# A hybrid decoder layer in Strassen products: weight sums on GpSimd, snapshots on VectorE, third products one pair later, last HGRN pieces between early products

## The chip, the cores and the metric

The kernel runs on one core of a Trainium2 chip. The metric is the device time of one execution in microseconds; the time before is the median of three runs. The engines go by the profile's names: PE is TensorE's matmuls, PEld its weight loads, DVE VectorE, ACT ScalarE, POOL GpSimd, SP SyncE, which here issues nearly all DMAs. Each engine works through its own queue in order, and an instruction that has to wait holds up what is queued behind it.

## The reference

One decoder layer on 1024 tokens of width 1024, all in float32. Three token mixers (an HGRN2 recurrence `o_a`, sliding-window attention `o_b`, attention to a memory `o_c`) read projections of h; each result goes through its own weight and a gate, and the sum through `w_out`:

```python
z = h @ w_in[layer]
...
gates = jax.nn.sigmoid(gl.astype(jnp.float32).reshape(B, S, N_BRANCHES, D_MODEL))
merged = (gates[:, :, 0] * (o_a @ w_branch_hg[layer])
          + gates[:, :, 1] * (o_b @ w_branch_swa[layer])
          + gates[:, :, 2] * (o_c @ w_branch_mem[layer]))
mix = merged @ w_out[layer]
h = layer_norm(alpha * h + mix, ln1_g[layer], ln1_b[layer])
ff = jnp.square(jax.nn.relu(h @ w_up[layer])) @ w_down[layer]
h = layer_norm(alpha * h + ff, ln2_g[layer], ln2_b[layer])
```

The change concerns two stages: the part of `h @ w_in` that makes the three gates and HGRN's output gate (the gate stage), and the three products `o @ w_branch` with their gates (the branch stage).

## The kernel before

**Products.** A float32 matrix is held as two parts, a high one that ScalarE casts (`split`, L77) and a low one, the rest, that GpSimd or VectorE subtracts (L78). A product of matrices is high times high, high times low and low times high. The large products use Strassen's scheme in Winograd's form: a weight of two 128x1024 pieces gives four quarter matrices, the activation gives seven operands `xs[1]` to `xs[7]` by sums of its quarters (`combine`, L200 to L210), and seven block products take the place of eight. `prod` (L285) is one block product: four k-steps of three matmuls of 128x512, twelve in all, into a PSUM bank. In the profile operands 1 and 2 lie in tiles X, 3 and 5 in O, 4 in T, 6 in MG and 7 in BT; weights in W, raw loads in R, PSUM banks in pz (three), ps (three) and pt (two). There are four R and four W buffers.

**A pair.** `prepare` (L328) loads two raw weight pieces and makes four sums of their halves on VectorE (`add`, L301), between them the splits of w2, w4 and w3, and of w1 where products 1 and 2 have not been made ahead. The sums are chained: a later one reads what an earlier one wrote. `run` (L341) then issues five or seven products. Bank pz takes product 1 (w1), 6 (w4) and 7 (w3) on top of each other; after each a copy of the running value is kept, by ScalarE (`snap`, L297), or by VectorE where a copy of product 1 is reloaded and added (`plus`). Bank pt takes product 5 (w2), is read by `emit(3)`, and takes product 3 (w3) on top for `emit(2)`. Bank ps takes product 4, and product 2 for `emit(0)`. So the third product on pt must wait until VectorE has read pt.

**Early products.** `two` (L318) makes products 1 and 2 of a weight ahead of the pairs; they need operands 1 and 2 alone. In the gate stage (L409 to L415) there are EARLY_Z = 10 of them, with `x_rest` (L219) between them, which loads pieces of x and makes operands 3 to 7 on VectorE; product 1's copy is stored to DRAM and reloaded. Sixteen pairs follow, the first ten with five products. In the branch stage (L888 to L914) each of three branches begins with EARLY_B = 3 of them, whose pz banks are held, then come four pairs (five products in three, seven in the last). `load_op` (L742) loads and splits the operands 3 to 7 of the branch, two loads of 512 KB for each, and operands 1 and 2 of the next branch at its end. In the first branch `job` (L422) also makes the operands of HGRN's output with `combine` on GpSimd, one job after each pair.

**Emit.** In the branches an `emit` (L860 to L886) reads the PSUM bank with the copy (VectorE, L301), loads the gate, multiplies (L874 in the first branch, L876 later) and adds to the running sum (L301).

**The HGRN tail.** Each head of HGRN is a row of steps; `heads[7][3]`, `heads[6][4]` and `heads[7][4]` (L833 to L835) are the last of a half: a head's output product with its mask, and two ends with a normalisation on VectorE and transposes on PE.

**What sets the order.** A tile scheduler orders each engine's instructions from the program's order, the dependences and the buffers; the queues that come out are those shown with the change.

## Time and profile before

| | us |
|---|---|
| median of three runs (2227.44 to 2231.4) | 2228.95 |
| the profiled execution | 2228.37 |
| its span, first to last instruction | 2226.6 |
| gate stage, early products (56.0 to 145.8) | 89.8 |
| gate stage, five-product pairs (145.8 to 274.3) | 128.5 |
| first branch (1136.3 to 1235.2) | 98.9 |
| second branch (1235.2 to 1336.4) | 101.2 |
| third branch (1336.4 to 1434.9) | 98.5 |

The stretches were read from PE's timeline. In a row of a timeline, consecutive matmuls of one kind are joined (x12 is one product); what stands in brackets is the idle time of the engine ahead of it and the instruction whose end released it. Matmul ends are modelled, so the distance from one start to the next says more than the length of a row.

### The profile page before, as it was taken

To read this page: it belongs to the slowest core of one execution; us is meant where nothing else is said; L and a number is where in the kernel's file an instruction comes from. 1 tells how busy PE (TensorE), PEld (TensorE's weight loads), DVE (VectorE), ACT (ScalarE), POOL (GpSimd) and SP (SyncE) were. 2 spreads that over 40 slices of the span, in tenths; PEclk is the share of its full clock that TensorE was granted. 3 is DMA by queue.
4 is the path that set the end of the run, shared out by engine and by line. 5 is a ranking of instruction groups with operands and counts; after the bars stand their busy time and mean duration, and the time that the engine had idled before them with its cause. 6 is when DMAs were issued, how large, how long until landed. Compare 5 with 4: busy or idle time off the path is not lost.

```text
span 2226.6 us, 27069 instructions
## 1 busy us (share of the span) xinstructions
PE 2061.4 (93%) x9906; PEld 1681.2 (76%) x9906; DVE 1418.6 (64%) x2218; ACT 883.7 (40%) x1546; POOL 938.2 (42%) x430
## 2 busy tenths in 40 slices
PE   8889999999999999999978797898989999999987
PEld 8667788777789877779956575777778887788865
DVE  5634435576445577575574778845556655588898
ACT  5433333444444344454321433413544455433321
POOL 2533333211222222423355545634533334777674
PEclk9999999999999999999989898999899999999998
DMA  8554434322234323554355646435556546744322
GB/s 286 192 170 144 135 105 128 115 85 83 98 108 129 114 91 113 186 202 166 110 189 212 239 146 218 155 113 180 194 183 228 187 155 211 289 152 151 114 86 76
DMA packets 153781, 347.03 MB, mean 156 GB/s; under 512 B 13696, under 2 KB 31280, under 8 KB 153648
## 3 DMA queue, kind: packets, MB, share of 16 engines
q1 hardware_dynamic: 153040, 343.19, 46.4%
q10 hardware_dynamic: 608, 2.11, 0.3%
q8 instruction: 78, 1.28, 0.2%
q14 instruction: 55, 0.45, 0.1%
HBM read 254.01 MB, written 91.24 MB: 155 GB/s over the span
## 4 chain that ended last, share of the span: by engine, by line
PE 40%; DVE 7%; POOL 6%; DMA 5%; issue 5%; ACT 2%; SPq 0%; POOLq 0%; DVEq 0%; ACTq 0%
PE pz L62 20%; PE ps L62 12%; PE pt L62 7%; POOL W L78 2%; DMA R<-d_o 1%; DMA R<-in_w_up_dram 1%; DVE R L301 1%; DMA R<-in_w_b_dram 1%; DVE S L876 1%; DVE T L301 1%; POOL BT L78 1%; ACT W L77 1%; DVE G L301 1%; DMA S<-d_z 1%; POOL MG L78 0%
## 5 line engine op out<-in xcount | busy, mean ns | idle before, releaser
L78 POOL TENSOR_TENSOR W<-R,W 128x1024 fp32r<-128x1024 f32 x200 | 494.3, 2473 | 931.5 <-ACT W L77 890.1
L77 ACT CAST W<-R 128x1024 fp32r<-128x1024 f32 (+1 forms) x289 | 283.9, 983 | 378.4 <-DVE R L301 182.1
L62 PE MATMUL pz<-X,W 128*128 128x512 f32 x1344 | 338.2, 404 | 15.8 <-POOL W L78 5.6
L62 PEld LDWEIGHTS pz<-X,W 128*128 128x128 f32 x1344 | 256.4, 194 | 75.6 <-POOL W L78 9.5
L62 PE MATMUL pt<-O,W 128*128 128x512 f32 x1056 | 273.9, 409 | 36.4 <-DVE G L301 22.4
L62 PEld LDWEIGHTS pt<-O,W 128*128 128x128 f32 x1056 | 204.7, 197 | 93.1 <-DVE G L301 26.5
L62 PE MATMUL pz<-O,W 128*128 128x512 f32 x816 | 197.2, 395 | 0.0
L301 DVE TENSOR_TENSOR R<-R,R 128x512 f32<-128x512 f32 x132 | 102.6, 782 | 139.6 <-POOL W L78 113.3
L62 PEld LDWEIGHTS pz<-O,W 128*128 128x128 f32 x816 | 150.5, 188 | 32.2
L62 PE MATMUL pz<-MG,W 128*128 128x512 f32 x528 | 134.6, 400 | 15.1 <-ACT W L77 13.3
L62 PE MATMUL pz<-BT,W 128*128 128x512 f32 x528 | 131.5, 398 | 14.0 <-DVE G L301 13.6
L62 PEld LDWEIGHTS pz<-MG,W 128*128 128x128 f32 x528 | 101.6, 194 | 40.5 <-ACT W L77 15.5
L62 PE MATMUL ps<-X,W 128*128 128x512 f32 x528 | 129.2, 393 | 2.3 <-DVE G L301 2.3
L62 PEld LDWEIGHTS pz<-BT,W 128*128 128x128 f32 x528 | 99.3, 191 | 40.8 <-ACT W L77 15.8
L62 PE MATMUL ps<-T,W 128*128 128x512 f32 x528 | 129.1, 392 | 0.1
L62 PEld LDWEIGHTS ps<-X,W 128*128 128x128 f32 x528 | 99.9, 190 | 24.3 <-DVE G L301 3.1
L62 PEld LDWEIGHTS ps<-T,W 128*128 128x128 f32 x528 | 99.9, 189 | 21.7 <-ACT T L77 0.6
L78 DVE TENSOR_TENSOR W<-R,W 128x512 fp32r<-128x512 f32 (+1 forms) x91 | 92.8, 1020 | 22.1 <-ACT W L77 21.8
L78 POOL TENSOR_TENSOR MG<-R,MG 128x1024 fp32r<-128x1024 f32 (+1 forms) x39 | 100.6, 2582 | 12.6 <-ACT MG L77 12.6
L78 POOL TENSOR_TENSOR BT<-R,BT 128x1024 fp32r<-128x1024 f32 x31 | 82.8, 2673 | 51.5 <-ACT BT L77 51.5
L301 DVE TENSOR_TENSOR T<-pt,G 128x512 f32<-128x512 f32 x64 | 44.0, 688 | 66.9 <-PE pt L62 62.4
L297 ACT COPY G<-pz 128x512 f32<-128x512 f32 x92 | 53.4, 581 | 78.1 <-PE pz L62 78.1
(289 smaller groups left out, 3712.5 us busy)
## 6 DMA issues: line engine op xcount, KB each, us to landing
R<-d_ff SPq DMA_DIRECT2D x49, 512.0 KB, 3.7
R<-in_w_up_dram SPq DMA_DIRECT2D x42, 512.0 KB, 4.1
R<-in_w_gate_dram SPq DMA_DIRECT2D x34, 512.0 KB, 4.0
R<-in_w_b_dram SPq DMA_DIRECT2D x33, 512.0 KB, 4.3
d_ff<-T SPq DMA_DIRECT2D x56, 256.0 KB, 3.1
d_z<-T SPq DMA_DIRECT2D x54, 256.0 KB, 2.5
R<-d_o SPq DMA_DIRECT2D x26, 512.0 KB, 3.8
d_o<-G SPq DMA_DIRECT2D x48, 256.0 KB, 2.3
```

Source lines behind the costliest of these rows:

```text
L62: nc.tensor.matmul(o, lhsT=l, rhs=r, start=start, stop=stop, skip_group_check=more)
L77: (hi_copy or nc.scalar.copy)(hi, src)
L78: (lo_eng or nc.gpsimd).tensor_tensor(out=lo, in0=src, in1=f32(hi), op=ALU.subtract)
L297: nc.scalar.copy(t, o)
L301: nc.vector.tensor_tensor(out=o, in0=a_, in1=b_, op=op)
L876: nc.vector.scalar_tensor_tensor(out=th, in0=th, scalar=1.0, in1=v, op0=ALU.add, op1=ALU.mult)
```

## The change

In the gate and branch stages the copies of pz are taken by VectorE (`copy_out`) in place of ScalarE. The four sums of `prepare` go from VectorE to GpSimd. In `run` the order of products becomes 6, 4, 7, 5, and product 3 with `emit(2)` is kept as `late` and issued in the next pair: after its product 1, or ahead of its product 6; in a `two`, between its two products. EARLY_Z becomes 12, `x_rest` comes after early products 2, 4, 6 and 8 (counted from 0) in place of 1, 3, 5 and 7. In the branches the emit of product 4, now the first after product 7, takes a tile of its own, in place of the emit of product 5. The three HGRN pieces of the second half come one behind each of the first branch's three early products; this branch's operands are loaded behind them. The jobs of the first branch are cut in two of 256 columns each, which take one R tile in place of two and are both run behind the next pair. The diff, cut to its core:

```diff
-EARLY_Z = 10
+EARLY_Z = 12
...
+    def copy_out(o):
+        t = st("G", [P, TH])
+        nc.vector.tensor_copy(t, o)
+        return t
+    late = [None]
+    def finish_late():
+        if late[0]:
+            late[0]()
+            late[0] = None
     def two(src, keep, emit):
...
         prod(o, w1, 0, 1)
+        finish_late()
         s1 = keep(o)
...
-        add(r0[:, L], r0[:, L], r1[:, L], ALU.subtract)
-        add(r1[:, L], r1[:, L], r1[:, H])
+        def sub(o, a_, b_, op=ALU.subtract):
+            nc.gpsimd.tensor_tensor(out=o, in0=a_, in1=b_, op=op)
+        sub(r0[:, L], r0[:, L], r1[:, L])
+        sub(r1[:, L], r1[:, L], r1[:, H], ALU.add)
         w2 = halves(r1, nc.gpsimd)
-        add(r1[:, H], r1[:, H], r0[:, L], ALU.subtract)
+        sub(r1[:, H], r1[:, H], r0[:, L])
...
-        add(r0[:, H], r0[:, H], r1[:, H], ALU.subtract)
+        sub(r0[:, H], r0[:, H], r1[:, H])
...
-            s1 = snap(o)
+            s1 = copy_out(o)
+        finish_late()
...
-        s2 = snap(o) if p1 is None else plus(o, p1)
+        s2 = copy_out(o) if p1 is None else plus(o, p1)
+        c = pt("s")
+        prod(c, w2, 1, 4)
+        prod(o, w3, 0, 7, False)
+        s3 = copy_out(o) if p1 is None else plus(o, p1)
+        emit(1, c, s3)
         b_ = pt("t")
         prod(b_, w2, 0, 5)
-        prod(o, w3, 0, 7, False)
-        s3 = snap(o) if p1 is None else plus(o, p1)
         emit(3, b_, s3)
-        c = pt("s")
-        prod(c, w2, 1, 4)
-        emit(1, c, s3)
-        prod(b_, w3, 1, 3, False)
-        emit(2, b_, s2)
+        def rest():
+            prod(b_, w3, 1, 3, False)
+            emit(2, b_, s2)
+        late[0] = rest
...
-        if i % 2 and i < 8:
-            x_rest(i // 2)
+        if i in (2, 4, 6, 8):
+            x_rest(i // 2 - 1)
...
+    def half_job(br, k, c):
+        t = st("R", [P, 2, 2, 256])
+        for e in range(2):
+            nc.sync.dma_start(t[:, e], d_o[br, k + 4 * e].rearrange("p (h t) -> p h t", h=2)[:, :, c:c + 256])
+        def part(j, src, e):
+            if j != 3:
+                nc.sync.dma_start(d_c[br, j - 4, k, :, c:c + 256], src)
...
-            v = st("G", [P, TH]) if b == 3 else s_
+            v = st("G", [P, TH]) if b == 1 else s_
...
-            banks.append(two(w[2 * i], snap, b_emit(e, i)))
+            banks.append(two(w[2 * i], copy_out, b_emit(e, i)))
+            if e == 0:
+                (heads[7][3], heads[6][4], heads[7][4])[i]()
...
+        if e == 0:
+            operand_tiles()
+            load_op(br, 6)
+            ws = prepare(w[0], w[1], False)
+            load_op(br, 4)
+        for j in (7, 5, 3):
             load_op(br, j)
...
-                if todo:
+                while todo:
                     todo.pop(0)()
-                todo.append(job(0, i, nc.gpsimd, [st("R", [P, S]) for _ in range(2)]))
+                for c in (0, 256):
+                    todo.append(half_job(0, i, c))
```

How the queues change, at three places. VectorE, in the gate stage, around the copies of one pair with a reloaded product 1, before:

```order
L301 TENSOR_TENSOR T_1160<-pt_1133,G_1131 128x512
L301 TENSOR_TENSOR R_1293<-R_1293,R_1291 128x512
L301 TENSOR_TENSOR R_1291<-R_1291,R_1293 128x512
L301 TENSOR_TENSOR G_1227<-pz_1214,G_1212 128x512
L78 TENSOR_TENSOR W_1301<-R_1293,W_1301 128x512
L301 TENSOR_TENSOR R_1387<-R_1387,R_1389 128x512
L301 TENSOR_TENSOR R_1389<-R_1389 128x512
L301 TENSOR_TENSOR G_1254<-pz_1214,G_1212 128x512
L301 TENSOR_TENSOR T_1256<-pt_1229,G_1254 128x512
L301 TENSOR_TENSOR T_1256<-ps_1260,G_1254 128x512
L301 TENSOR_TENSOR T_1256<-pt_1229,G_1227 128x512
```

and after:

```order
L301 TENSOR_TENSOR T_1236<-pt_1240,G_1207 128x512
L301 TENSOR_TENSOR G_1303<-pz_1275,G_1273 128x512
L78 TENSOR_TENSOR W_1362<-R_1354,W_1362 128x512
L301 TENSOR_TENSOR G_1330<-pz_1275,G_1273 128x512
L301 TENSOR_TENSOR T_1332<-ps_1305,G_1330 128x512
L301 TENSOR_TENSOR T_1332<-pt_1336,G_1330 128x512
L301 TENSOR_TENSOR T_1332<-pt_1336,G_1303 128x512
L301 TENSOR_TENSOR G_1399<-pz_1371,G_1369 128x512
L78 TENSOR_TENSOR W_1458<-R_1450,W_1458 128x512
L301 TENSOR_TENSOR G_1426<-pz_1371,G_1369 128x512
```

The four sums on R have left VectorE's queue; the half subtraction of w4 (L78) stays, and the emit of ps comes ahead of those of pt.

PE, at the seam of two five-product pairs of the gate stage, before (pt_1229 is the first pair's bank, pz_1310 the next pair's):

```order
L62 MATMUL ps_1260<-T_117,W_1201 128x512 x2
L62 MATMUL ps_1260<-T_118,W_1201 128x512
L62 MATMUL ps_1260<-T_117,W_1201 128x512
L62 MATMUL pt_1229<-O_111,W_1209 128x512 x12
L62 MATMUL pz_1310<-MG_113,W_1301 128x512
L62 MATMUL pz_1310<-MG_114,W_1301 128x512
```

and after (pt_1336 the first pair's, pz_1371 the next pair's):

```order
L62 MATMUL pz_1275<-BT_115,W_1270 128x512
L62 MATMUL pt_1336<-O_112,W_1262 128x512 x12
L62 MATMUL pz_1371<-MG_113,W_1362 128x512
L62 MATMUL pz_1371<-MG_114,W_1362 128x512
L62 MATMUL pz_1371<-MG_113,W_1362 128x512 x2
L62 MATMUL pt_1336<-O_111,W_1270 128x512 x12
L62 MATMUL pz_1371<-MG_114,W_1362 128x512
```

Before, product 3 (O_111) follows product 4, three products behind product 5 of its bank. After, product 5 (O_112) and product 3 stand four matmuls of the next pair apart.

PE, at the end of HGRN and the first early products of the branches (pz_9223 is the first one's bank; T_8367, BT_8969, cst belong to HGRN), before:

```order
L62 MATMUL ps_9162<-T_8367,S_9142 128x128 x4
L62 MATMUL ps_9178<-T_8367,con 128x128 x4
L62 MATMUL ps_9178<-BT_8969 128x128
L62 MATMUL pz_9223<-X_9005,W_9220 128x512
L62 MATMUL pz_9223<-X_9004,W_9220 128x512 x2
L729 MATMUL pt_9202<-cst,S_9048 128x128
L62 MATMUL ps_9178<-BT_8969 128x128
L729 MATMUL pt_9202<-cst,S_9048 128x128 x3
L62 MATMUL ps_9178<-BT_8969 128x128
L62 MATMUL pz_9223<-X_9005,W_9220 128x512
L62 MATMUL pz_9223<-X_9004,W_9220 128x512 x2
```

and after (ps_9275 is product 2 of the second early weight, pz_9304 product 1 of the third, L764 the transposes of a head's end):

```order
L62 MATMUL ps_9275<-X_9018,W_9257 128x512 x2
L62 MATMUL ps_9275<-X_9019,W_9257 128x512
L62 MATMUL ps_9275<-X_9018,W_9257 128x512
L764 MATMUL pt_9292<-cst,S_9062 128x128 x4
L62 MATMUL pz_9304<-X_9018,W_9301 128x512
L62 MATMUL pz_9304<-X_9019,W_9301 128x512
L62 MATMUL pz_9304<-X_9018,W_9301 128x512 x2
```

Before, the head pieces lie within the first early product; after, each lies behind the second product of a pair of early ones.

## Rows read from the trace of the kernel before

**Rows 1.** Page, part 1: busy us of each engine, share of the span, instructions.

```profile
PE 2061.4 (93%) x9906; PEld 1681.2 (76%) x9906; DVE 1418.6 (64%) x2218; ACT 883.7 (40%) x1546; POOL 938.2 (42%) x430
```

**Rows 2.** Stretches: PE, PEld, DVE, ACT, POOL busy (count); PE clock, DMA share, GB/s.

```profile
56.00:145.80 89.80, 73.45 (x291) 57.78 (x291) 47.53 (x54) 35.16 (x54) 41.17 (x19) 0.90 0.56 188
145.80:274.30 128.50, 125.15 (x541) 100.48 (x540) 57.92 (x88) 39.58 (x54) 45.54 (x19) 1.00 0.44 142
1136.30:1235.20 98.90, 81.61 (x313) 64.95 (x312) 55.25 (x52) 26.78 (x33) 57.61 (x30) 0.86 0.61 218
1235.20:1336.40 101.20, 86.92 (x338) 65.51 (x337) 76.60 (x74) 36.14 (x43) 48.68 (x20) 0.93 0.55 187
1336.40:1434.90 98.50, 82.73 (x338) 65.25 (x337) 81.45 (x78) 41.22 (x55) 53.27 (x22) 0.91 0.56 181
```

**Rows 3.** Timeline of PE, up stage: start, us, instruction [idle before <-releaser].

```profile
1660.96 1.07 PE L62 MATMUL pz<-MG,W 128*128 128x512 f32 x4
...
1674.84 1.07 PE L62 MATMUL pz<-MG,W 128*128 128x512 f32 x4
```

**Rows 4.** Timeline of PE and DVE, a five-product pair of the gate stage.

```profile
195.11 1.42 DVE L301 TENSOR_TENSOR R<-R,R 128x512 f32<-128x512 f32 x2 [2.91 <-POOL W L78]
...
197.28 3.01 PE L62 MATMUL pz<-BT,W 128*128 128x512 f32 x12 [0.37 <-DVE G L301]
```

**Rows 5.** Timeline of PE and DVE, start of the gate stage.

```profile
92.99 5.49 PE L62 MATMUL pz<-X,W 128*128 128x512 f32 x12 [2.58 <-ACT G L297]
...
137.40 5.46 PE L62 MATMUL pz<-BT,W 128*128 128x512 f32 x12 [7.72 <-DVE G L301]
...
135.24 1.41 DVE L301 TENSOR_TENSOR R<-R,R 128x512 f32<-128x512 f32 x2
```

**Rows 6.** Timeline and waits of PE, first early products of the branches.

```profile
1112.78 1.17 PE L62 MATMUL pz<-X,W 128*128 128x512 f32 x4
...
1135.52 1.09 PE L729 MATMUL pt<-cst,S 128*128 128x128 f32 x4 [5.39 <-DVE S L723]
1136.26 4.38 PE L62 MATMUL pz<-X,W 128*128 128x512 f32 x10
...
1148.68 2.88 PE L62 MATMUL pz<-MG,W 128*128 128x512 f32 x12
...
PE pt L729 <- DVE S L723: 8.0, 2, 5.4
PE ps L62 <- DVE con L687: 3.1, 1, 3.1
```

**Rows 7.** Timeline of POOL and DVE in the same stretch.

```profile
1129.57 2.35 POOL L78 TENSOR_TENSOR W<-R,W 128x1024 fp32r<-128x1024 f32 x1
1129.64 2.31 DVE L1224 TENSOR_TENSOR sm<-sm 128x4 f32<-128x4 f32 x1 [1.12 <-POOL sm L1223]
```

**Rows 8.** Waits in the branches (1136.3 to 1434.9): us in total, times, longest.

```profile
ACT G L297 <- PE pz L62: 38.7, 17, 7.9
...
PE pt L62 <- DVE G L301: 22.4, 9, 6.3
```

**Rows 9.** DVE's groups, gate pairs (146 to 274): count, busy us, mean ns.

```profile
L301 DVE TENSOR_TENSOR R<-R,R 128x512 f32<-128x512 f32 x26 | 18.0, 690 | 29.6 <-POOL W L78 29.3
```

**Rows 10.** The same view, branches, DVE and POOL.

```profile
L301 DVE TENSOR_TENSOR R<-R,R 128x512 f32<-128x512 f32 x35 | 36.6, 1046 | 37.7 <-POOL W L78 30.0 <-DMA R<-in_w_b_dram 7.4
...
L301 DVE TENSOR_TENSOR G<-pt,G 128x512 f32<-128x512 f32 x23 | 15.7, 683 | 8.7 <-ACT G L297 5.8 <-PE pt L62 2.9
...
L78 POOL TENSOR_TENSOR W<-R,W 128x1024 fp32r<-128x1024 f32 x32 | 79.7, 2495 | 104.8 <-ACT W L77 104.8
```

**Rows 11.** Instructions of single lines: ns min/median/max, first and last start.

```profile
L203 POOL TENSOR_TENSOR R<-R x4: 1283/1292/1334, 1157.5 to 1210.8; 128x512 f32<-128x512 f32 x4
...
L207 POOL TENSOR_TENSOR R<-R,R x4: 1300/1596/1597, 1162.4 to 1216.2; 128x512 f32<-128x512 f32 x4
...
L876 DVE SCALAR_TENSOR_TENSOR S<-S,G x32: 676/693/2886, 1243.7 to 1448.9; 128x512 f32<-128x512 f32 x32
```

More of the change, by code (lines that the diff above doesn't have):

```diff
@@ L345, in run @@
             prod(o, w1, 0, 1)
-            s1 = snap(o)
+            s1 = copy_out(o)
+        finish_late()
+        if w1 is not None:
             d = pt("s")
@@ L430, in job @@
         return lambda: combine([v[:, 0:TH] for v in t], [v[:, TH:S] for v in t], part, eng)
+    def half_job(br, k, c):
[5 more added lines that the diff above has]
+                nc.sync.dma_start(d_c[br, j - 4, k, :, c:c + 256], src)
+        return lambda: combine([t[:, e, 0] for e in range(2)], [t[:, e, 1] for e in range(2)], part, nc.gpsimd)
     jt = []
@@ L891, in hybrid_layer @@
         banks = []
+        ws = None
         for i in range(EARLY_B):
[L893 removed]
+            banks.append(two(w[2 * i], copy_out, b_emit(e, i)))
+            if e == 0:
+                (heads[7][3], heads[6][4], heads[7][4])[i]()
             if i == 0:
[L895 to L899 removed]
+                if e:
+                    operand_tiles()
+                    load_op(br, 6)
+            elif i == 1 and e:
+                ws = prepare(w[0], w[1], False)
+                load_op(br, 4)
+        if e == 0:
+            operand_tiles()
+            load_op(br, 6)
+            ws = prepare(w[0], w[1], False)
+            load_op(br, 4)
+        for j in (7, 5, 3):
             load_op(br, j)
```

18 lines of the change are left out of this document (8 added, 10 removed).

## The prediction

> **What bounds the kernel now.** I read the page first: over the whole span TensorE (PE) is busy 93%, VectorE (DVE) 64%, GpSimd (POOL) 42%, ScalarE (ACT) 40% [rows 1]. That average hides the stages, so next I read the stretches that the change touches [rows 2]. Five of them matter: the start of the gate stage (89.8 us, PE busy 73.45, clock 0.90), its five-product pairs (128.5 us, PE 125.15, clock 1.00), and the three branches (98.9, 101.2 and 98.5 us, PE busy 81.61, 86.92 and 82.73, clock 0.86 to 0.93). The 128.5 us of pairs are bound by PE. The start and the branches are not: there something else decides, and PE loses twice, in idle time and in the lower granted clock behind it.
>
> What a full product costs: twelve 128x512 matmuls. In the up stage, which this change leaves alone and which already defers its third products, five products come round every 13.88 us (1660.96 to 1674.84) without a wait, 2.78 each [rows 3]. A branch has three pairs of five products, one of seven and three pairs of early products, 28 products: 28 x 2.78 = 77.7 us. So the second and third branch lose about 22 us each, and the first, which starts ahead of its stretch, about as much. That is where a gain, and a loss, can be.
>
> **The gate stage's pairs.** Each pair of five products holds a wait of 0.37 us ahead of its product on BT, which ends on VectorE's sum G [rows 4]. The row beside it says why: at 195.11 VectorE makes two of prepare's sums (1.42 us), and only behind them, in 0.68, the G for which PE waits at 197.28. The change sends these sums to GpSimd. The up stage's rhythm of 13.88 is then what remains: ten pairs x 0.37 = -3.7 us. EARLY_Z 12 turns two of the six seven-product pairs into five-product pairs with two early products ahead: the same matmuls at another place, 0 us, with two more stores and two more loads of 256 KB. What hides GpSimd's sums: a pair there has two half-subtractions of 2.40 us (19 of them make 45.5 us in 128.5 [rows 2]) and gets four sums of about 1.3 us (their price stands below), 10 us of 13.9. If that cover is thin, the four sums and the cast behind them are late for the next pair; I keep +8 us as the upper bound. Taken: **-4 us** (-5 to +8).
>
> **The start of the gate stage.** PE waits 2.58 us ahead of 92.99 (ScalarE's snapshot) and 7.72 us ahead of 137.40, and the twelve matmuls behind each take 5.49 and 5.46 us instead of about 2.9, since the clock had fallen [rows 5]. The long wait ends on VectorE's G of pair 0, which is queued behind the sums of pair 2 that wait for their weights: two of them, at 135.24, are the last ahead of it [rows 5]. With the sums on another queue that G comes as soon as its product has ended. But the row speaks only of the last link: x_rest(3), loaded two early products later in the new order, with three instead of two pairs of early products behind it, must still make operand 7 (BT). The whole wait and its slow product are 7.7 + 2.6 = 10.3 us; nothing of it is the one bound, all of it and the 2.58 the other. The snapshots now stand in VectorE's queue between x_rest's subtractions, which wait for their loads; that is a reason for a loss of up to 4. I take half: **-5 us** (-13 to +4).
>
> **The last HGRN results.** In the kernel before, the last three head pieces run in one go: from the first early product of the branches (1112.78) to the first pair (1148.68) it takes 35.9 us [rows 6], for six products of 2.78 = 16.7 us and the small matmuls. Within it PE waits 5.39 us for VectorE ahead of 1135.52, and the ten matmuls behind take 4.38 us instead of 2.3. Two rows show what VectorE did meanwhile: a TENSOR_TENSOR on 128x4 elements lasts 2.31 us, from 1129.64 to the end of GpSimd's 2.35 us subtraction of 1129.57 [rows 7]. The change puts one piece behind each of the three pairs of early products: 5.5 us of matmuls lie under each wait. If all the waits (8.0 us on S with the 5.39 in it, 3.1 on con [rows 6]) and the 2.1 of the slow matmuls were covered, 35.9 would become 35.9 - 11.1 - 2.1 = 22.7. Against that: operand 6 (MG) of the first pair is loaded behind the early products instead of among them, two loads, two casts and two subtractions of 2.4 us, some 10 us from issue to ready, and the last piece still has VectorE's chain under it. I take 26: **-10 us** (-13 to 0).
>
> **The branches.** Taken away: PE's waits for VectorE's sum ahead of third products, 22.4 us in nine waits [rows 8]. They arise because the third product adds to the bank that emit(3) must read first. The deferral puts four MG matmuls, 0.9 us, between the two; the read itself is 0.68 us [rows 10]. That is thin, yet in the up stage the same order runs without a wait [rows 3]. Taken away as well: ScalarE's snapshots, which made it wait 38.7 us for PE with casts queued behind them [rows 8].
>
> Added: four sums per pair move from VectorE to GpSimd. On VectorE an undisturbed one takes 0.69 us (26 of the gate stage, mean 690 [rows 9]); on GpSimd no sum of two weight halves is in the trace, and the nearest rows are HGRN's combines of the same shape in the first branch, 1.28 us at the least and 1.29 or 1.60 in the median of a line [rows 11]. Why this counts although neither engine is full: the two do not overlap freely. In [rows 7] VectorE is held to the end of GpSimd's instruction, and L876, with two operands in SBUF, goes from 0.68 to 2.89 us [rows 11], while sums that read PSUM stay at a mean of 683 ns [rows 10]. So I cost the time that both together need: 12 pairs x 4 x (1.29 - 0.69) = 28.8 us. Half jobs: 32 operations on 256 columns for 16 on 512. No 256-column row exists; with 128x1024 at 2.40 and 128x512 at 1.29 a line gives about 0.75: 32 x 0.75 - 16 x 1.29 = +3.4 us, with bounds of 0.65 (+0.2) and 1.29 (+21). The snapshots on VectorE read PSUM and add nothing there. The 24 extra DMA issues lie on SP beside compute; in the worst case they delay a weight load by a few us once per pair of the first branch. Sum: -22.4 + 28.8 + 3.4 = **+10 us** (-20 with ScalarE's decoupling worth a third of the lost 66 us and the sums hidden, to +32 with no wait saved).
>
> **Sum.** -4 - 5 - 10 + 10 = -9 us against the profiled execution of 2228.37 us: 2219.4. The median of the runs lies 0.6 above that execution, so 2220 us.
>
> **Rivals.** *The shared access decides the branches (slower).* A five-product pair of the second or third branch needs, in time in which only one of the two works: two subtractions on GpSimd (2 x 2.40), four sums (4 x 0.69 before), VectorE's half subtraction (0.69), and L876 and a running sum for each of three results (6 x 0.69): 12.4 us before, and with the sums at 1.29 it is 14.8, the subtractions for operands on top in both. From the point where this exceeds the 13.88 us of PE's five products the branch goes at the pace of the two engines and no saved wait comes back: +32 in place of +10, so -19 + 32 = +13, 2242 us. For it: GpSimd's subtractions in the branches average 2.50 us, not 2.40, and VectorE's sums there 1046 ns, not 690 [rows 9, 10]. Against it: in the third branch GpSimd is busy 53 of 98.5 us and VectorE 81 [rows 2], not all of it exclusive. The Trainium skill's "GPSIMD Engine Reference" speaks against the change here, twice: under "Engine selection" an elementwise sum belongs on VectorE, GpSimd being about twice as slow with two inputs, and under "Specifications" the two share SBUF interfaces, with contention where VectorE reads two inputs from SBUF. The trace agrees with both (1.29 against 0.69; 2.31 us for a 128x4 operation). Taken alone the page would have the sums stay where they are, and this rival come true.
>
> *Decoupling pays (faster).* VectorE's long queue of the branches held casts up: GpSimd waited 104.8 us for ScalarE's casts [rows 10], and these for the sums. With sums and subtraction in one queue, and ScalarE left with casts alone, weights are ready a pair ahead, and the branches get back a third of what they lose now, as above: -20 in place of +10, in sum -39, 2190 us.
>
> *The moves change nothing.* The load of operand 6 behind the early products takes the place of the tail's wait, 0 instead of -10: -4 - 5 + 10 = +1, 2230 us.
>
> **How the numbers follow.** Forecast 0.42, shared access 0.27, decoupling 0.18, no change 0.13. The forecast's own range is 2209 to 2230. For 8 in 10, the range takes in the nearer halves of both outer rivals: 2188 to 2252. About 0.2% (4.5 us) is what a measurement can tell from no change: faster (below 2224.5) 0.36 of the forecast and all of decoupling, 0.54; within it 0.05 + 0.11 + 0.02 = 0.18; slower 0.01 + 0.02 + 0.25 = 0.28.
>
> **What would show it.** Gate pairs at 13.9 us without the 0.37; the wait ahead of pair 0 under 4 us; first early product of the branches to the first pair about 26 us; waits of third products for G gone or short; sums on GpSimd at 1.3 us. For the shared access: branches of 104 us and more, with VectorE's instructions on SBUF at 1.5 to 3 us and PE waiting for weights of GpSimd. For decoupling: branches near 90 us at a clock over 0.95. The forecast is wrong first where the branches move by more than 10 us either way.

## The result, and the profile after

The changed kernel takes 2258.25 us (median of four runs, 2257.0 to 2265.8), the kernel before 2228.39 beside it: a ratio of 1.0139, 95% interval 1.0114 to 1.0164. It is slower by 31 us (1.39% of 2228), where 2220 was forecast, and outside the range of 2188 to 2252.

The page's first lines, to be read against [rows 1]: the span, then each engine's busy time.

```profile
span 2257.7 us, 27177 instructions
...
PE 2071.4 (92%) x9906; PEld 1686.8 (75%) x9906; DVE 1388.3 (61%) x2170; ACT 850.8 (38%) x1482; POOL 1095.8 (49%) x558
```

VectorE does less (1388 us against 1419), ScalarE less (851 against 884), GpSimd 158 us more, and PE's 9906 matmuls 10 us more in all. The stretches of the changed kernel (columns as in [rows 2]: PE, PEld, DVE, ACT and POOL busy, PE clock, DMA share, GB/s) are the start of the gate stage, ten of its pairs, and the three branches:

```profile
55.90:145.40 89.50, 75.45 (x314) 59.54 (x312) 51.29 (x55) 31.52 (x45) 50.68 (x28) 0.96 0.61 201
145.40:274.30 128.90, 127.66 (x554) 103.20 (x555) 42.31 (x56) 40.24 (x55) 96.18 (x57) 1.00 0.44 147
1133.60:1237.10 103.50, 72.15 (x267) 54.04 (x265) 47.10 (x50) 21.34 (x22) 72.28 (x56) 0.85 0.65 207
1237.10:1350.90 113.80, 88.79 (x325) 68.23 (x326) 73.22 (x65) 31.38 (x32) 75.13 (x37) 0.84 0.52 168
1350.90:1468.00 117.10, 94.52 (x355) 71.60 (x354) 89.36 (x80) 34.31 (x42) 80.17 (x39) 0.90 0.48 162
```

In the gate stage PE has done 314 matmuls after 89.5 us where it had done 291 after 89.8, at a clock of 0.96 instead of 0.90. 23 matmuls of 0.23 us are 5 us. PE's timeline shows the pairs (start, us, instruction, and in brackets the idle time ahead and what ended it):

```profile
134.47 5.88 PE L62 MATMUL pz<-MG,W 128*128 128x512 f32 x12 [5.96 <-ACT W L77]
...
145.44 3.02 PE L62 MATMUL pz<-BT,W 128*128 128x512 f32 x12 [2.32 <-DVE G L301]
...
166.44 1.07 PE L62 MATMUL pz<-MG,W 128*128 128x512 f32 x4
...
180.22 1.07 PE L62 MATMUL pz<-MG,W 128*128 128x512 f32 x4
```

From 166.44 to 180.22 a pair takes 13.78 us, without the wait of 0.37 of [rows 4]. Ahead of the first pair PE waits 5.96 us for the cast of its weight and 2.32 for BT, where [rows 5] showed 7.72 for BT alone. The stage ends 10.2 us earlier than before, counted from its first product (344 us against 354). The heads between it and the branches take 6.3 us longer (708.8 us against 702.5; 704 to 714 in the traces of the other runs), which no run explains. At the HGRN pieces, from the first early product of the branches to the first pair, the 35.9 us of [rows 6] have become 25.0:

```profile
1108.62 1.17 PE L62 MATMUL pz<-X,W 128*128 128x512 f32 x4
...
1115.64 4.61 PE L62 MATMUL ps<-X,W 128*128 128x512 f32 x12 [3.05 <-DVE sm L1273]
...
1133.64 2.54 PE L62 MATMUL pz<-MG,W 128*128 128x512 f32 x10
```

So the forecast's terms of -4, -5 and -10 are there, each at its place, though 6.3 us of them are gone by the first early product of the branches. The loss is in the branches. From the first pair's first product to the first product on MG of the stage that follows, before and then after:

```profile
1148.60:1436.10 287.50, 240.16 (x944) 186.72 (x943) 207.35 (x194) 98.69 (x123) 156.77 (x70) 0.91 0.57 195
```

```profile
1133.60:1468.00 334.40, 255.46 (x945) 193.87 (x944) 209.67 (x193) 87.02 (x96) 227.58 (x131) 0.86 0.55 178
```

287.5 us have become 334.4, 47 more. (Counted from the first early product, with the HGRN pieces in it, 323.4 have become 359.5, 36 more: the 11 us gained at the pieces are given back too.) Two parts of it can be read off these two lines: PE idle, 287.5 - 240.2 = 47.3 before and 78.9 after, 31.6 more; and 15.3 more for the same matmuls (944 and 945), at a granted clock of 0.86 instead of 0.91. Who made PE wait, in the changed kernel (us in total, times, longest):

```profile
ACT W L77 <- POOL R L346: 125.6, 27, 11.5
...
PE pz L62 <- ACT W L77: 25.1, 6, 12.2
PE pt L62 <- DVE G L301: 19.4, 8, 4.1
...
PE ps L62 <- ACT W L77: 8.9, 2, 6.3
PE pz L62 <- DVE G L320: 8.9, 5, 3.6
```

PE's waits for VectorE's sums ahead of third products, 22.4 us in [rows 8], are still 19.4, and 8.9 for VectorE's copies have come to them. PE's waits for casts of weights have grown to 34 us (before 10.4 on pz and 7.8 on pt), and behind them ScalarE waits 125.6 us for GpSimd's sums.

### The profile page after: what moved, and what is told of

The parts are those of the page before. It is cut to its first block, busy times and chain, and to the rows that moved or that the text cites. A ratio compares the mean times of both kernels' runs of the same rounds, so it can differ in the third digit from the quotient of the medians.

```text
span 2257.7 us, 27177 instructions
## 1 busy us (share of the span) xinstructions
PE 2071.4 (92%) x9906; PEld 1686.8 (75%) x9906; DVE 1388.3 (61%) x2170; ACT 850.8 (38%) x1482; POOL 1095.8 (49%) x558
## 4 chain that ended last, share of the span: by engine, by line
PE 34%; DVE 9%; POOL 8%; DMA 7%; issue 6%; ACT 3%; SPq 0%; POOLq 0%; DVEq 0%; ACTq 0%
PE pz L62 17%; PE ps L62 11%; PE pt L62 5%; POOL W L78 4%; POOL R L346 2%; DMA R<-in_w_b_dram 1%; DMA R<-in_w_up_dram 1%; ACT W L77 1%; DMA R<-d_o 1%; DVE T L301 1%; DVE S L912 1%; DMA R<-d_ff 1%; DVE W L78 1%; DVE R L301 1%; DVE S L301 1%
## 5 line engine op out<-in xcount | busy, mean ns | idle before, releaser
L78 POOL TENSOR_TENSOR W<-R,W 128x1024 fp32r<-128x1024 f32 x200 | 494.6, 2474 | 780.8 <-ACT W L77 689.6
L62 PE MATMUL pt<-O,W 128*128 128x512 f32 x1056 | 269.9, 406 | 21.5 <-DVE G L301 19.4
L78 DVE TENSOR_TENSOR W<-R,W 128x512 fp32r<-128x512 f32 (+1 forms) x91 | 106.6, 1172 | 111.8 <-ACT W L77 110.2
L62 PE MATMUL pz<-MG,W 128*128 128x512 f32 x528 | 144.0, 414 | 23.6 <-ACT W L77 20.2
L62 PE MATMUL pz<-BT,W 128*128 128x512 f32 x528 | 132.3, 399 | 14.8 <-DVE G L320 7.0
L62 PEld LDWEIGHTS pz<-MG,W 128*128 128x128 f32 x528 | 103.5, 199 | 52.9 <-ACT W L77 23.1
L346 POOL TENSOR_TENSOR R<-R,R 128x512 f32<-128x512 f32 x84 | 118.6, 1422 | 39.1 <-DMA R<-in_w_b_dram 20.3
L78 POOL TENSOR_TENSOR BT<-R,BT 128x1024 fp32r<-128x1024 f32 x31 | 82.1, 2652 | 61.8 <-ACT BT L77 61.8
L78 POOL TENSOR_TENSOR MG<-R,MG 128x1024 fp32r<-128x1024 f32 (+1 forms) x39 | 100.6, 2583 | 14.4 <-ACT MG L77 14.4
L62 PE MATMUL ps<-W,BT 128*128 128x512 f32 x264 | 68.8, 392 | 10.5 <-POOL BT L78 7.1
```

What stands on the lines that cost most here:

```text
L62: nc.tensor.matmul(o, lhsT=l, rhs=r, start=start, stop=stop, skip_group_check=more)
L78: (lo_eng or nc.gpsimd).tensor_tensor(out=lo, in0=src, in1=f32(hi), op=ALU.subtract)
L346: nc.gpsimd.tensor_tensor(out=o, in0=a_, in1=b_, op=op)
```

## The experiments

Each run was timed in three rounds against the kernel before on the same chip. The branch stage is measured in the profiled execution, on PE's timeline, as above: from the first pair's first product to the first product on MG behind the branches and their last third product (in b_copies, late_only and s_psum one to three matmuls of that product slip ahead of the third product; there the rest of it counts). Most runs of one kernel lie within 10 us of their median, one of b_jobs 14 us above it, and the kernel before took 2225.8 to 2228.2 us beside the others, so the ratios and their intervals count. A difference of two ratios is known to some 4 to 10 us. The profiled execution lay 5 to 9 us below the median in b_copies, late_only, b_all, no_sums, d_chain, s_psum and order_tail, so a single stage time is read with that in mind.

| kernel | median us | ratio to before, 95% | branch stage us |
|---|---|---|---|
| before | 2228.4 | 1 | 287.5 |
| changed | 2258.3 | 1.0114 to 1.0164 | 334.4 |
| b_sums | 2235.1 | 1.0012 to 1.0043 | 310.3 |
| b_copies | 2253.9 | 1.0097 to 1.0153 | 326.2 |
| b_order | 2250.6 | 1.0085 to 1.0131 | 320.2 |
| b_jobs | 2248.1 | 1.0067 to 1.0141 | 324.7 |
| late_only | 2231.2 | 1.0010 to 1.0045 | 307.8 |
| b_all | 2223.9 | 0.9966 to 0.9995 | 292.8 |
| no_sums | 2218.8 | 0.9935 to 0.9969 | 289.1 |
| d_load | 2275.9 | 1.0208 to 1.0250 | 349.5 |
| d_load2 | 2274.8 | 1.0190 to 1.0245 | 352.2 |
| d_memset | 2233.2 | 1.0009 to 1.0040 | 310.7 |
| d_chain | 2247.8 | 1.0069 to 1.0130 | 320.4 |
| s_sbuf | 2249.5 | 1.0078 to 1.0121 | 327.2 |
| s_psum | 2249.7 | 1.0071 to 1.0118 | 321.8 |
| sums_alone | 2234.0 | 1.0012 to 1.0041 | 297.2 |
| gate_only | 2221.2 | 0.9973 to 0.9998 | 281.5 |
| gate_sums | 2220.5 | 0.9952 to 0.9976 | 288.2 |
| gate_order | 2216.5 | 0.9926 to 0.9959 | 287.3 |
| order_tail | 2219.5 | 0.9953 to 0.9977 | 289.5 |

### One part undone in the branches

**b_sums.** In the changed kernel:

```diff
-def prepare(src0, src1, first):
+def prepare(src0, src1, first, branch=False):
...
-            nc.gpsimd.tensor_tensor(out=o, in0=a_, in1=b_, op=op)
+            (nc.vector if branch else nc.gpsimd).tensor_tensor(out=o, in0=a_, in1=b_, op=op)
```

> The changed kernel with the four sums of prepare back on VectorE in the branch stage alone; the gate stage keeps them on GpSimd, and copies, order, jobs and loads stay as changed. Theory A (the sums on GpSimd, through the access it shares with VectorE and its own longer queue, cost the branches their 46 us): the branches get most of it back, 30 us or more, so about 2225 us, and VectorE's own instructions on SBUF come back to about 1.1 us in the mean. Theory B (VectorE's queue with the copies in it is what holds PE up): VectorE gets more work still, the time stays at 2258 or rises. Theory C (order, half jobs or moved loads): no more than 10 us of change.

Measured 2235.1: 23 us come back, less than the 30 of theory A, and against theory B. A sum of two raw halves takes 828 ns in the mean on VectorE (undisturbed ones and others together), and 1438 on GpSimd in the changed kernel. First VectorE's group in b_sums (count, busy us, mean ns, idle ahead), then GpSimd's in the changed kernel:

```profile
L346 DVE TENSOR_TENSOR R<-R,R 128x512 f32<-128x512 f32 x33 | 27.3, 828 | 29.8 <-POOL W L78 25.7 <-DMA R<-in_w_b_dram 3.9
```

```profile
L346 POOL TENSOR_TENSOR R<-R,R 128x512 f32<-128x512 f32 x33 | 47.3, 1438 | 21.7 <-DMA R<-in_w_b_dram 17.5 <-DVE G L301 2.7
```

**b_copies.** In the branches:

```diff
-            banks.append(two(w[2 * i], copy_out, b_emit(e, i)))
+            banks.append(two(w[2 * i], snap, b_emit(e, i)))
...
-        s3 = copy_out(o) if p1 is None else plus(o, p1)
+        s3 = (snap if branch else copy_out)(o) if p1 is None else plus(o, p1)
```

> The changed kernel with the copies of pz back on ScalarE in the branch stage alone. Theory A: little, within 6 us of 2258, since copies that read PSUM do not need the shared access. Theory B: VectorE's queue loses 34 copies of 0.68 us, and PE's waits for them (8.9 us) go; 15 us or more come back, about 2243.

2253.9, 4 us less: within what theory A allowed, and far from theory B's 15. The two intervals overlap for most of their width, so it is not shown that the copies cost anything.

**b_order.** In the branches:

```diff
+        if branch:
+            prod(o, w4, 0, 6, p1 is not None)
+            s2 = copy_out(o)
+            b_ = pt("t")
+            prod(b_, w2, 0, 5)
+            prod(o, w3, 0, 7, False)
+            s3 = copy_out(o)
+            emit(3, b_, s3)
+            c = pt("s")
+            prod(c, w2, 1, 4)
+            emit(1, c, s3)
+            prod(b_, w3, 1, 3, False)
+            emit(2, b_, s2)
+            return
...
-            v = st("G", [P, TH]) if b == 1 else s_
+            v = st("G", [P, TH]) if b == 3 else s_
```

> The changed kernel with the order of products and emits of before in the branch stage alone (third products not deferred there). Theory A: within 6 us of 2258. Theory C in its form that the deferral holds banks of pt and weights in W a pair longer and so delays the next casts: 15 us or more come back, about 2243. Against both: the waits of third products on VectorE grow again, up to 20 us, 2275.

2250.6, 8 us less: neither within theory A's 6 nor theory C's 15, and at the edge of what the intervals can tell from nothing. The trace answers the rival "against both". PE's waits in b_order's branches:

```profile
PE pz L62 <- ACT W L77: 40.3, 7, 16.0
...
PE pt L62 <- DVE G L301: 3.4, 4, 1.5
```

With third products not deferred, their waits for VectorE's sums fall from 19.4 us to 3.4, and the waits on pz for casts rise from 25.1 to 40.3. A wait that goes at one place comes back at another, as long as the weights come late.

**b_jobs.**

```diff
-                for c in (0, 256):
-                    todo.append(half_job(0, i, c))
+                todo.append(job(0, i, nc.gpsimd, [st("R", [P, S]) for _ in range(2)]))
```

> The changed kernel with the full jobs of before in the first branch. In the changed kernel PE waits 12 us at the end of the first branch for a weight, behind operand loads that come 24 us late in SP's queue, with the stores of the last half jobs issued ahead of them. If the half jobs are the cause, 8 us or more come back, 2250 or less; if any job at that place does it, it stays within 5 us of 2258. By my price for the half jobs (3 us) it would be 2255.

2248.1, 10 us less by the medians, but the interval overlaps that of the changed kernel: the gain is not clear of the scatter. What the half jobs do is seen at the end of the first branch, in the changed kernel's timeline of SP's queue, ScalarE and PE:

```profile
1217.22 5.87 SPq L463 DMA_DIRECT2D d_c<-R  x7
...
1223.15 1.48 SPq L89 DMA_DIRECT2D R<-d_o  x3
...
1228.04 1.04 ACT L77 CAST X<-R 128x1024 fp32r<-128x1024 f32 x1 [23.67 <-DMA R<-d_o]
...
1237.12 1.22 PE L62 MATMUL pz<-X,W 128*128 128x512 f32 x2 [12.16 <-ACT W L77]
```

SP issues seven stores of half jobs for 5.87 us, and only then, at 1223.15, the loads of the next branch's operands. ScalarE has waited 23.67 us when the first has landed, and PE 12.16 us when the next weight, queued behind these operands' casts, is ready. The computing was priced well (0.73 us for an undisturbed half, estimated 0.75); the queue of SP was named in the forecast, with a few us at the worst, and stood in its sum with nothing. But the 12.16 us are not what the half jobs cost. In b_jobs, whose full jobs have half as many stores, ScalarE's wait there is 14.28 us and PE stands at nearly the same place for VectorE's sum:

```profile
1227.97 4.09 PE L62 MATMUL pt<-O,W 128*128 128x512 f32 x10 [9.96 <-DVE G L301]
```

Its first branch, from the first pair to the next branch's first product, takes 99.3 us against 103.5: 4 us at this place.

**b_all and late_only.** b_all has sums, copies, order, jobs and operand loads of the branches as before; late_only has sums on VectorE, copies on ScalarE and full jobs, and keeps the deferral, the loads' new order and the moved HGRN pieces.

> The changed kernel with sums, copies, order, jobs and operand loads of the branch stage as before; what stays of the change is the gate stage and the HGRN pieces among the early products. If the gains read from the trace (10 us in the gate stage, 11 at the pieces, some 6 lost again within the heads ahead of them) stand by themselves, it takes 2228 - 10 - 5 = 2213 us, and the whole loss lies in the other edits of the branch stage. If the moved pieces themselves delay the branches, it stays above 2225.

> The changed kernel with sums on VectorE, copies on ScalarE and full jobs in the branches; the deferred third products, the new order of loads and the moved HGRN pieces stay. If undoing parts adds up (23 for the sums, 4 for the copies, some for the jobs), 2228 or less; if the deferral itself is what remains of the loss, it stays 6 us or more above the run with the whole branch stage as before (2224).

b_all takes 2223.9, 34 us less than the changed kernel, so the whole loss lies in the branch stage's own edits; but it is 11 us above the 2213 expected. late_only takes 2231.2, 7 us above it, with intervals that do not meet: the deferral and the moved loads cost something in the branches even alone. The single parts undone give 23 + 4 + 8 + 10 = 45 us, more than the 34 of all together; but three of the four are no larger than their uncertainty, so it is not shown that the parts overlap.

### What GpSimd's time costs there, and why

**no_sums.**

```diff
-            nc.gpsimd.tensor_tensor(out=o, in0=a_, in1=b_, op=op)
+            if not branch:
+                nc.gpsimd.tensor_tensor(out=o, in0=a_, in1=b_, op=op)
```

> The changed kernel with the four sums of prepare left out in the branches (the weights there are then the raw halves). It gives the whole price of the sums at either place: the sums on GpSimd cost what lies between this and 2258, on VectorE what lies between this and 2235. If the sums on VectorE were hidden, it stays at 2235; if both engines' time is paid for as in the other runs (0.4 to 0.6 us per us), 2220 or less.

2218.8, for a kernel that leaves out the sums in the branches and so computes something else. So the sums cost 39 us on GpSimd and 16 on VectorE: neither place is free, and GpSimd's is the dearer by 23.

**sums_alone.** The other way round: the branch stage of before, with the sums on GpSimd and nothing else changed in it (gate stage as in gate_sums, below).

> The branch stage of before with its sums on GpSimd and nothing else changed in it, and the gate stage of the run with sums back on VectorE there (2220.5). Undone from the changed kernel, the sums' place was worth 23 us. If it is a price of its own, 2243 here too. If it is one only together with the copies on VectorE and the deferral, 2230 or less; if it pays alone, less than 2220.

2234.0 against gate_sums' 2220.5, +13.5: a price of its own, but less than the 23 that it costs beside the copies, the deferral and the half jobs.

**d_load.** On top of b_sums:

```diff
+        w3 = halves(r0, nc.gpsimd)
+        if branch:
+            for _ in range(4):
+                nc.gpsimd.tensor_tensor(out=w4[:, 0, H], in0=f32(w4[:, 0, L]), in1=f32(w4[:, 1, L]), op=ALU.subtract)
-        return w1, w2, w4, halves(r0, nc.gpsimd)
+        return w1, w2, w4, w3
```

**d_chain.** On top of b_sums, each cast of w2, w4 and w3 is done twice in the branches, for w4 thus:

```diff
+        if branch:
+            nc.scalar.copy(w4[:, 0, L], r1[:, H])
         split(w4[:, 0, L], w4[:, 1, L], r1[:, H], nc.vector)
```

> The run with sums on VectorE in the branches (2235), with four operations of 128x512 with two SBUF operands added on GpSimd behind each of the 12 pairs' w4, whose output goes to an unused half of w4's tile: the load of the four sums on GpSimd and on the shared access, without their place between a weight's load and its casts. Theory A1 (the access that the two engines share decides: time used on it is paid for): 48 x 1.29 = 62 us more of it, PE pays at least as much as for the moved sums, 2258 or more. Theory A2 (the chain from a load over the sums and casts to the product has become longer, and the four raw buffers let no load start earlier): no more than 8 us, about 2240.

> The run with sums on VectorE in the branches (2235), with each cast of w2, w4 and w3 made twice on ScalarE in the branches: 1.05 + 0.62 + 1.05 us more per pair between a weight's load and its product, on an engine that is not on the shared access and is idle two thirds of the time. The sums on GpSimd lengthened the same chain by four times 0.75 us. Theory A2: 20 us or more, 2255. Theory A1: within 6 us of 2235.

d_load: 2275.9, 41 us more than b_sums, as the shared access would have it. d_chain: 2247.8, 13 us more, between its two theories: a longer chain from load to product is paid for too, at less than half of the 32 us that it adds. d_load has a flaw, in GpSimd's group of the added operations (busy, mean | idle ahead of them):

```profile
L358 POOL TENSOR_TENSOR W<-W 128x512 fp32r<-128x512 f32 x44 | 65.2, 1483 | 26.8 <-DVE W L78 24.8
```

GpSimd stood 24.8 us in these operations waiting for VectorE's half subtraction of w4. d_load2 takes that away.

**d_load2** reads w2's parts, which GpSimd itself has just written; **d_memset** has eight memsets in place of the four operations (d_load2, then d_memset, against d_load):

```diff
-                nc.gpsimd.tensor_tensor(out=w4[:, 0, H], in0=f32(w4[:, 0, L]), in1=f32(w4[:, 1, L]), op=ALU.subtract)
+                nc.gpsimd.tensor_tensor(out=w4[:, 0, H], in0=f32(w2[:, 0, L]), in1=f32(w2[:, 1, L]), op=ALU.subtract)
...
-            for _ in range(4):
+            for _ in range(8):
-                nc.gpsimd.tensor_tensor(out=w4[:, 0, H], in0=f32(w4[:, 0, L]), in1=f32(w4[:, 1, L]), op=ALU.subtract)
+                nc.gpsimd.memset(f32(w4[:, 0, H]), 0.0)
```

> As d_load, but the four added operations of GpSimd per pair read w2's two parts, which GpSimd itself has just written, so that its queue waits for no other engine there (in d_load it waited 25 us for VectorE's half subtraction of w4). If operations with two operands in SBUF cost by themselves, through the shared access, what memsets of nearly the same busy time did not (d_memset, 2233), then 2255 or more. If the 41 us of d_load were its wait for VectorE and not the load, 2242 or less.

> The run with sums on VectorE in the branches (2235), with eight memsets of 128x512 on GpSimd per pair into the unused half of w4's tile: time in GpSimd's queue that reads nothing from SBUF, against the four two-operand operations of d_load (65 us busy, 2276). If GpSimd's queue is what the load costs, it loses by the same rate, 0.6 us per us of added busy time, so some 25 us or more for 40 us and more of it (2260). If the shared access for reading is what it costs, VectorE's operations are not stretched by it and it stays within 8 us of 2235.

d_load2 takes 2274.8, so it was the load and not the wait. d_memset takes 2233.2, not slower than b_sums. The branches of b_sums, d_memset and d_load2 (columns as in [rows 2]):

```profile
1133.30:1443.60 310.30, 244.90 (x946) 188.62 (x945) 225.13 (x237) 88.38 (x98) 168.41 (x87) 0.90 0.60 193
```

```profile
1135.10:1445.80 310.70, 244.26 (x945) 188.80 (x944) 217.97 (x237) 88.32 (x98) 203.17 (x175) 0.90 0.59 192
```

```profile
1130.00:1482.30 352.30, 256.63 (x946) 196.10 (x945) 253.47 (x237) 88.22 (x98) 236.53 (x131) 0.85 0.52 171
```

GpSimd is busy 203 us with the memsets and 237 with the operations that read, instead of 168; VectorE is busy 218 and 253 instead of 225, for the same 237 instructions. The loads on GpSimd's queue are thus not equal, 35 us more against 68. At d_load2's rate, 40 us for 68, the 35 would have cost 20, and they cost nothing. The added operations of d_memset, then of d_load2 (ns min/median/max), and two groups of VectorE in d_load2:

```profile
L358 POOL MEMSET W<- x96: 516/526/532, 1121.2 to 1418.6; 128x512 f32 x96
```

```profile
L358 POOL TENSOR_TENSOR W<-W x48: 1265/1598/2124, 1115.2 to 1454.0; 128x512 fp32r<-128x512 f32 x48
```

```profile
L346 DVE TENSOR_TENSOR R<-R,R 128x512 f32<-128x512 f32 x33 | 39.2, 1187 | 28.4 <-POOL W L78 25.9 <-DMA R<-in_w_b_dram 2.3
...
L78 DVE TENSOR_TENSOR W<-R,W 128x512 fp32r<-128x512 f32 x11 | 15.4, 1402 | 0.0
```

The memsets take 516 to 532 ns whatever VectorE does; the operations that read two tiles 1265 to 2124. VectorE's sums go from 828 ns in b_sums to 1187 beside the latter, its half subtraction of w4 from 975 to 1402. One stretch of d_memset's timeline shows the difference on one engine:

```profile
1274.89 2.72 POOL L78 TENSOR_TENSOR W<-R,W 128x1024 fp32r<-128x1024 f32 x1 [3.91 <-ACT W L77]
...
1275.31 2.85 DVE L916 SCALAR_TENSOR_TENSOR S<-S,G 128x512 f32<-128x512 f32 x1
...
1277.55 3.45 POOL L358 MEMSET W<- 128x512 f32 x6
1278.08 0.68 DVE L346 TENSOR_TENSOR R<-R,R 128x512 f32<-128x512 f32 x1
1278.68 0.68 DVE L301 TENSOR_TENSOR T<-T,S 128x512 f32<-128x512 f32 x1
```

Beside GpSimd's subtraction (1274.89) VectorE's L916, with two operands in SBUF, lasts 2.85 us, to 0.55 us behind the subtraction's end; beside six memsets (from 1277.55) the same kind of operation lasts 0.68. So time in GpSimd's queue does not cost by itself; what costs goes with reading on GpSimd while VectorE wants two operands from SBUF. This agrees with what the Trainium skill's "GPSIMD Engine Reference" states under "Specifications", that the two share SBUF interfaces. That a load on the queue costs only from some amount above the memsets' on, 4.2 us a pair, is not excluded.

**s_sbuf and s_psum.** On top of b_sums, four operations per pair on VectorE ahead of the emit of product 4, with two operands in SBUF, or, in s_psum, with product 4's bank in PSUM as the first (`in0=c`):

```diff
+        if branch:
+            for _ in range(4):
+                nc.vector.tensor_tensor(out=w4[:, 0, H], in0=f32(w4[:, 0, L]), in1=f32(w4[:, 1, L]), op=ALU.subtract)
         emit(1, c, s3)
```

> The run with sums on VectorE in the branches (2235), with four more VectorE operations of 128x512 per pair that read two operands in SBUF and write to the unused half of w4's tile: 48 x 0.69 = 33 us undisturbed. If the shared access decides, each costs the access and is stretched to about 1.2 us behind GpSimd: 25 us or more, 2260. If only GpSimd's own queue counts (the load of the run d_load stood in that queue), VectorE, busy some 70% there, takes it with 10 us or less, 2245.

> The same four operations with one of their operands read from product 4's PSUM bank, for the same time in VectorE's queue without the second operand in SBUF. If the shared access decides, they last 0.69 us each and cost half or less of what the run with two SBUF operands does. If VectorE's queue as such decides, both runs are within 5 us of each other.

VectorE's added operations in s_sbuf, then in s_psum (count | busy us, mean ns):

```profile
L376 DVE TENSOR_TENSOR W<-W 128x512 fp32r<-128x512 f32 x44 | 56.2, 1277 | 0.7
```

```profile
L376 DVE TENSOR_TENSOR W<-ps,W 128x512 fp32r<-128x512 f32 x47 | 32.3, 687 | 6.1 <-PE ps L62 5.3
```

Stretched to 1277 ns in the one, 687 in the other, as expected. But both kernels take 2249.5 us, 14 more than b_sums, and their branch stages are 17 and 12 us longer. By the expectation's own measure, both within 5 us of each other, this is the outcome in which VectorE's queue as such decides. The pair does not settle it, since the two sets stand at other places of the queue: in s_psum casts of weights wait for the added operations (this row of its branches; s_sbuf has none like it).

```profile
ACT W L77 <- DVE W L376: 31.4, 4, 8.7
```

What the second SBUF operand of VectorE's own operations costs the kernel in the end stays open.

### The gate stage and the HGRN pieces

**gate_only**: the change in the gate stage alone, with branches and HGRN pieces as before. **gate_sums**: the same with the sums on VectorE. **gate_order**: also with copies on ScalarE, so that EARLY_Z 12, the later x_rest, the order of products and the deferral are left. From the gate stage of the changed kernel to gate_order:

```diff
-            nc.gpsimd.tensor_tensor(out=o, in0=a_, in1=b_, op=op)
+            nc.vector.tensor_tensor(out=o, in0=a_, in1=b_, op=op)
...
-            s1 = copy_out(o)
+            s1 = snap(o)
...
-            t = copy_out(o)
+            t = snap(o)
```

> The kernel before with the change in the gate stage alone (sums, copies, deferred third products, EARLY_Z 12, x_rest later). The forecast's terms for it were -4 and -5, and the trace of the changed kernel shows 10 us less at the end of the stage: about 2218. If what is gained there is lost again in the stage behind it, 2226 or more.

> The run with the change in the gate stage alone (2221), with the sums back on VectorE there. By the forecast's reading the waits of 0.37 us per pair and a long wait ahead of pair 0's product on BT come back, with 4 to 10 us: 2225 to 2231. If the new order of the products alone took those waits away, it stays at 2221.

> The run with the change in the gate stage alone, with sums on VectorE and copies on ScalarE there as before: what stays is EARLY_Z 12, the later x_rest, the new order of products and the deferral. The run with sums back took 2220.5, not slower than 2221. If the order of products is what takes the 0.37 us waits away, 2220 again; if the copies on VectorE do, 2226 or more.

2221.2, 2220.5 and 2216.5: the last is the fastest of all, 0.9926 to 0.9959 of the kernel before. PE's timeline of gate_sums, the wait ahead of the first pair's BT and the seams of two pairs:

```profile
140.78 4.42 PE L62 MATMUL pz<-BT,W 128*128 128x512 f32 x12 [5.91 <-DVE G L301]
...
161.55 1.07 PE L62 MATMUL pz<-MG,W 128*128 128x512 f32 x4
...
175.35 1.07 PE L62 MATMUL pz<-MG,W 128*128 128x512 f32 x4
```

With the sums back on VectorE the wait of 0.37 does not come back: from 161.55 to 175.35 a pair takes 13.80 us. A long wait ahead of BT (5.91) stays, and yet the kernel is no slower. Counted as above, the gate stage takes 342.4 us in gate_sums and 340.4 in gate_order, against 343.9 in the changed kernel and 354.1 before: the whole gain is there without moving sums or copies.

**order_tail**: gate_order with the three HGRN pieces among the early products.

```diff
-        heads[7][3]()
-        heads[6][4]()
-        heads[7][4]()
+        if hf == 0:
+            heads[7][3]()
+            heads[6][4]()
+            heads[7][4]()
...
+            if e == 0:
+                (heads[7][3], heads[6][4], heads[7][4])[i]()
```

> The run gate_order (2216.5) with the three HGRN pieces moved among the early products and the branches as before. If the moved pieces gain by themselves what the trace shows at their place (11 us from the first early product to the first pair), 2208 to 2211. If the first branch gives it back, since its weights and operands come at the pace of its buffers and not of its start, 2214 or more.

2219.5, not faster than gate_order's 2216.5. At its place the move gains (28.3 us from the first early product to the first pair, against 34.2); the first branch behind it, to the next branch's first product, takes 89.1 us against 84.2. The two branches, gate_order's and then order_tail's:

```profile
1137.90:1222.00 84.10, 66.75 (x265) 53.07 (x264) 45.55 (x43) 20.67 (x26) 50.60 (x28) 0.90 0.64 219
```

```profile
1131.50:1220.60 89.10, 71.20 (x266) 55.59 (x265) 46.40 (x49) 24.83 (x30) 51.78 (x28) 0.86 0.68 225
```

PE is idle 17.4 us in the one and 17.9 in the other; 4.5 us of the difference are the same matmuls at a granted clock of 0.86 instead of 0.90.

## Why the prediction was wrong, step by step

**Gate stage, pairs (-4) and start (-5): right in size, wrong in cause.** The stage ends 10.2 us earlier, some 5 in its pairs and 5 at its start, so that the size is luck. The step read the 0.37 us as VectorE's two sums ahead of its G [rows 4] and credited their move. gate_sums and gate_order have the sums back and are as fast or faster. What is left in gate_order is EARLY_Z 12, the later x_rest, the new order and the deferral, which no run takes apart. For the 0.37 us the new order is the likely one: product 4 now lies between product 6 and product 7, for which VectorE's sum on the bank must be ready. The row showed what stood last in the queue, not what a different order of products would make of it. The bound of +8 for a thin cover on GpSimd was not needed.

**HGRN pieces (-10): right at their place, nothing in the sum.** 25.0 us was measured where 26 was forecast; order_tail shows that the kernel gains nothing from it. The forecast priced what speaks against it inside the piece alone, not in the branch behind it, which takes back 4.9 of the 6 us in order_tail. That the branch waits for its operands and weights there is not shown: PE's idle time is the same in both, and its clock is lower.

**Branches (+10): the step that failed.** Its sum was -22.4 + 28.8 + 3.4.

- The -22.4 did not come. PE waits 19.4 us for VectorE's sums of product 5 and 8.9 for its copies, 28.3 in all. The four MG matmuls that were to cover VectorE's read are often not there: in three of the eight waits (6.6 us) the third product stands directly behind product 5 in PE's queue, as here:

```profile
1215.81 2.88 PE L62 MATMUL pt<-O,W 128*128 128x512 f32 x12
1220.73 4.22 PE L62 MATMUL pt<-O,W 128*128 128x512 f32 x12 [2.04 <-DVE G L301]
```

In three more (10.9 us) five or six matmuls lie between and do not suffice. So the up stage's rhythm [rows 3], from which the forecast took that the deferral is enough, does not carry over. And by b_order these waits are no sum that can be taken away by itself. VectorE is held up as well: its L912 takes 1284 ns in the mean, before (L876) 1161, and 693 undisturbed [rows 11]:

```profile
L876 DVE SCALAR_TENSOR_TENSOR S<-S,G 128x512 f32<-128x512 f32 x30 | 34.8, 1161 | 4.8 <-DMA S<-d_z 4.3
```

```profile
L912 DVE SCALAR_TENSOR_TENSOR S<-S,G 128x512 f32<-128x512 f32 x31 | 39.8, 1284 | 3.0 <-issue 2.2
```

- The 28.8 for the sums was nearly right: 23 by b_sums, 13.5 by sums_alone. Its reason, the shared access, is what d_load2 and d_memset show. In the forecast it was set off against waits that stayed.
- The half jobs, +3.4, cost about 10 by the medians of b_jobs, with an interval that does not exclude 3.4, and 4 at the end of the first branch, where their stores stand in SP's queue ahead of the next branch's operands. The forecast named this queue and took it as nothing.
- Order and deferral were costed at a gain and gave none: they cost 8 us by b_order, at the edge of what can be told from nothing, and 7 together with the moved loads by late_only against b_all. The copies on VectorE were costed at nothing, and the 4 us of b_copies cannot be told from that.
- PE's clock was named ("PE loses twice") and then left out of every price. Of the 47 us, 15 are the same matmuls at a lower granted clock.

**The rivals.** "The shared access decides the branches" was nearest, and for reading on GpSimd d_load2 and d_memset bear its mechanism out. At 2242 it was 16 us short; it left out the clock and took the HGRN pieces as gained, and no run divides the 16 us. Its chance of 0.27 was too low; its own count, 14.8 us of exclusive time in a pair against PE's 13.88, with operand loads on top, already said that PE could not be kept fed. "Decoupling pays" is refuted: ScalarE, left with casts, waits 125.6 us for GpSimd's sums. The range's top of 2252 took +32 as the most that the branches could lose, while the worst row for each part (half jobs +21, sums at 1.60) and the clock were not added up.

**Open.** How much of VectorE's own time on SBUF is paid for in such a stage (s_sbuf and s_psum cost the same, for reasons that the pair does not separate), why the heads ahead of the branches take longer, and what order, copies and half jobs cost one by one.

## What to carry to other kernels

Before work moves from VectorE to GpSimd because neither is full (64% and 42% here), add up for one period of the loop the time in which GpSimd reads SBUF and the time in which VectorE reads two operands from SBUF; where the sum comes near the period of PE, expect the move to cost, and to cost PE's clock as well (here 14.8 us against 13.88, and a clock of 0.86 instead of 0.91). A gain at one place counts only if the stage behind it does not wait for something else: look there for what comes late next. And a wait that ends on an engine's last instruction does not say that this engine's queue is its cause; in the gate stage another order of PE's own products, with the deferral and the later loads, took it away without moving any work to another engine, and in the branches waits only moved from one place to another.

## What the runs showed of the hardware that was not expected

A memset of 128x512 on GpSimd takes 516 to 532 ns and shows no sign of being held up by VectorE or holding it up (VectorE is busy 218 us beside them, 225 without); the 96 of d_memset (50 us by their median) cost nothing that could be measured, the 48 operations of d_load2 that read two tiles (77 us by theirs) cost 40.
